# First S5 layer: block 0's table spread on TensorE, its loads first in GpSimd's queue, TensorE's opening in written order behind products of ones

## The chip, the cores and the metric

The kernel runs on one core of a Trainium2 chip. The metric is the device time of one execution in microseconds (us); the figure of a kernel is the median of its runs. The engines are TensorE (PE; its weight loads are PEld), VectorE (DVE), ScalarE (ACT), GpSimd (POOL) and SyncE (SP). SP issues most loads, GpSimd and ScalarE issue some, each in the order of its own queue.

## What is computed

A decoder trunk of four layers over 256 positions of width 1024. The token mixer of layers 0 and 3 is a diagonal complex state-space layer (S5), that of layer 1 attention with a forget gate, that of layer 2 gated linear attention. Each layer also has an MLP with squared ReLU and a gated per-layer embedding. Only the S5 layer at the start is touched:

```python
u = xn @ w_in                                  # xn = rmsnorm(h, norm_mix)
ab = exp(lam * dt)                             # complex, 64 groups x 64 states
coef = (ab - 1) / lam
x = einsum(u, coef * b)                        # into the states, per group of 16 channels
s = scan over time of s = ab * s + x
y = real(einsum(s, c)) + d_skip * u
z = gelu(y) @ w_glu;  h += ((z1 * sigmoid(z2)) @ w_out)
```

## The kernel before

All of it is float32. A float32 weight in `dense` is split by ScalarE into a rounded high part (`whi`) and by VectorE into a low part (`wlo`), and TensorE multiplies with both. In the first S5 layer the columns `u` are instead made with plain float32 products, which show as two records each in the trace.

The S5 layer treats four positions at a time. It has four *blocks* of 256 channels, and the work of block `b` is written as short steps, a letter and a number:

- `w(2b)`, `w(2b+1)`: the two halves of `u` of block `b`, eight products of 128x256 each. `w_in` comes in eight pieces (`halves`, loaded by `half` in turn into buffers named raw, wh, wl, so pieces 0, 3, 6 are named raw, pieces 1, 4, 7 wh, pieces 2, 5 wl). Odd pieces need the second half of the channels of x.
- `f(b)`: fetches the matrix b (`bT`) and the powers of `ab` for this block (`coef`, 64 copies of a small table spread over 128 partitions). The table is made once: VectorE computes `powers`, TensorE transposes them (`s5_table`), ScalarE copies them to the tile `ct`, four DMAs write `ct` to memory (`tab`), and two DMAs per block read it back spread out.
- `j(b)`: fetches `bc` (b and c for the way out).
- `i(b)`: VectorE multiplies bT with coef (`s5_in`: tiles `wh`, `wl`, three instructions, L865 to L867). `r(b)`: the rotation `rot`. `o(b)`, `k(b)`: the way out (`qo`, from `bc` and `cpow`) and the short-lag kernel `tm`, which goes through `kk` and DMAs.
- `u(b)`: VectorE scales the columns by the norm (`rstd`), and eight DMAs lay them out as `U`. `x(b)`: TensorE multiplies U with wh and wl, 64 written products. `s(b)`, `e(b)`: VectorE turns the result (tiles P, W, R) and scans. `y(b)`: TensorE adds tm, P and W parts. `t(b)`, `g(b)`: gelu and transposition.
- `d`, `l`, `a`, `b`: load and split pieces of `w_glu` and multiply the gate; `P`, `p`: products of the embedding (`praw`).

The norm needs the mean of squares: ScalarE makes `x` and `sq` of each of four pieces of h, TensorE adds them up (`mean`, L1258), VectorE adds epsilon (`rrow`, L337), GpSimd takes the power -0.5 (L341), VectorE makes `diag`, TensorE spreads it with a matrix of ones (L351), ScalarE copies it (`rstd`, L353).

The order on the engines is set by a scheduler with a simulated timeline: it takes the program's steps in the order of the strings FIRST and LATER as written and puts every instruction on its engine where that simulation has it ready. Two things bind it. `in_order` chains the instructions of the named engines inside its `with`. `keep_in_program_order` pins GpSimd's fetches. Buffers come from pools; "wt" (bT and coef) has four, "wk" in PSUM three.

Of the kernel before, what the change touches and what calls it, by code (L numbers as in the profile page):

```python
# [13 lines left out]
ALU = mybir.AluOpType  # L14
# [13 lines left out]
FIRST = """w2 w3 u0 r0 w4 i0 f2 x0 o0 j2 P0 k0 w5 u1 w6 s0 d0 e0 y0 r1 i1 f3 x1 t0 o1 j3 k1 g0 u2 w7 l0 P1 d1 s1 a0 p0 e1 y1 r2 i2 x2 t1 o2 k2 g1 u3 p1 p2 d2 p3 d3 l1 b0 l2 d4 a1  # L28
# [3 lines left out]


# [27 lines left out]
class Trunk:  # L61
# [767 lines left out]
    def s5_table(self, j, F):  # L829

        nc = self.nc
        ps = self.psum((128, 2, 128), "mk")
        nc.tensor.matmul(ps.rearrange("p i x -> p (i x)"), self.zero[:, 0:128], self.zero[:, 0:256], start=True, stop=True)
        for i in range(2):
            nc.tensor.transpose(ps[:, i, :], F[:, i].rearrange("x s p -> x (s p)"), self.ident)
        ct = self.a2("ct", (128, 2, 2, 64))
        nc.scalar.copy(ct.rearrange("x i g n -> x i (g n)"), ps)
        tab = self.dram.tile([2, 4, 4, 2, 8, 64], F32, name=f"tab{j}")
        for i in range(2):
            for g in range(2):  # L840
                nc.gpsimd.dma_start(tab[g, :, :, i].rearrange("s b p n -> (s b) p n"), ct[:, i, g, :])
        return tab


    def s5_fetch(self, j, tab, b, pin=lambda x: x):

        nc = self.nc
        bT, cf = (self.t4(n, (128, 2, 512), tag="wt") for n in ("bT", "coef"))
        pin(nc.gpsimd.dma_start(bT, self.A["s5_bT"][j, b]))
        for g in range(2):  # L850
            pin(nc.gpsimd.dma_start(cf[g * 64:(g + 1) * 64], tab[g, :, b].rearrange("s i p n -> s (i p n)").unsqueeze(0).broadcast_to([16, 4, 1024])))
        return bT, cf
# [6 lines left out]
    def s5_in(self, b, bT, cf, ahead=False):  # L859

        nc = self.nc
        if not ahead:
            w = [self.wp.tile([128, 2, 8, 64], F32, name=n, tag=n, bufs=BUFS[n]) for n in ("wh", "wl")]
            f = [t.rearrange("x i p n -> x i (p n)") for t in w]
            nc.vector.tensor_tensor(f[0], bT, cf[:, 0:1].broadcast_to([128, 2, 512]), ALU.mult)  # L865
            nc.vector.tensor_tensor(f[1][:, 0], bT[:, 0], cf[:, 1], ALU.mult)
            nc.vector.scalar_tensor_tensor(f[1][:, 1], bT[:, 1], -1.0, cf[:, 1], ALU.mult, ALU.mult)  # L867
            return [[w[0][:, 0], w[1][:, 1]], [w[1][:, 0], w[0][:, 1]]]
# [172 lines left out]
    def s5_ahead(self, l):  # L1041
# [8 lines left out]
        made = *self.s5_fetch(j, tab, 0), self.s5_fetch_out(j, 0)  # L1050
        yield
        parts = None
        for b in range(4):
# [9 lines left out]
            if b < 3:  # L1063
                made = *self.s5_fetch(j, tab, b + 1), self.s5_fetch_out(j, b + 1)
# [24 lines left out]
    def s5_start(self, l):  # L1089
# [7 lines left out]
        us, parts, rots, ins, outs, xs, states, Gs, units, bcs = ({} for _ in range(10))  # L1097
# [143 lines left out]
        if first:  # L1241
            halves = [self.raw0] + [self.half(w_in, i) for i in range(1, 8)]
            x = [self.t4("x", (128, 4, T), tag="x4") for _ in range(2)]
            x = [x[k // 4][:, k % 4] for k in range(8)]
            scalars, v["ms"] = self.s5_scalars(j), self.psum((128, 2))
# [15 lines left out]
            with self.in_order(mybir.EngineType.Activation):  # L1261
# [17 lines left out]
            run("f0 j0 f1 j1")  # L1279
            q.update(drain(scalars))  # L1280
            z(1)
            run("w1")
# [99 lines left out]
```

## Time and profile before

| | us |
|---|---|
| median of 3 runs | 1466.18 |
| lowest, highest | 1463.03, 1469.08 |
| profiled execution | 1464.28 |
| its span, first to last instruction | 1462.6 |
| first S5 layer, its block work on VectorE | about 31.5 to 126 of the span |
| TensorE busy, share of the span | 1400.6, 96% |
| VectorE, ScalarE, GpSimd busy | 1046.0, 717.6, 102.4 |

The profiled execution is 1.9 us below the median, and 1.7 us lie outside its span. Its mean granted TensorE clock is 0.985. Rows of the timeline give start, length, engine, line, operation, and in brackets the idle time ahead and what ended it.

### The profile page before, as it was taken

What the parts mean: (1) busy time and instruction counts of PE and PEld (TensorE: products, weight loads), DVE (VectorE), ACT (ScalarE), POOL (GpSimd) and SP (SyncE); (2) the same over time, 40 slices, a digit from 0 to 9 for tenths busy, and PEclk for the clock granted to TensorE, in tenths of its full rate; (3) what the DMA queues carried; (4) which work ended last, traced back from release to release, by engine and by line L of the source; (5) the groups of instructions that cost most, each with busy time, mean ns of one, the idle gap of its engine ahead of it and who ended that gap; (6) DMA issues with size and microseconds to landing.
All of it is one profiled execution on the core that took longest, in us unless ns stands there. A gap on an engine that the chain in (4) does not pass through costs nothing.

```text
span 1462.6 us, 26508 instructions
## 1 busy us (share of the span) xinstructions
PE 1400.6 (96%) x10718; PEld 1261.5 (86%) x10718; DVE 1046.0 (72%) x1651; ACT 717.6 (49%) x1117; POOL 102.4 (7%) x169
## 2 busy tenths in 40 slices
PE   8789999999999999999999999999997899999997
PEld 7688988888999888888989588888997799888897
DVE  7894678776777678786676468877676946766664
ACT  3224465454655665455566445455463345545453
POOL 3000000001010000100004000000002100000020
PEclk9999999999999999999999999999999899999999
DMA  7533556657554456765665445666656546566561
GB/s 259 151 104 113 179 170 201 188 162 223 177 150 145 121 167 189 251 211 178 188 181 155 130 129 187 196 210 191 216 161 206 175 148 185 176 185 197 174 191 58
DMA packets 143387, 255.06 MB, mean 174 GB/s; under 512 B 21680, under 2 KB 32272, under 8 KB 143264
## 3 DMA queue, kind: packets, MB, share of 16 engines
q1 hardware_dynamic: 129856, 227.66, 50.3%
q0 software_dynamic: 7520, 24.26, 4.9%
q10 hardware_dynamic: 5888, 1.44, 0.5%
q8 instruction: 84, 1.38, 0.4%
q14 instruction: 39, 0.32, 0.1%
HBM read 242.68 MB, written 7.86 MB: 171 GB/s over the span
## 4 chain that ended last, share of the span: by engine, by line
PE 59%; DMA 4%; DVE 3%; ACT 3%; issue 1%; POOL 1%; DVEq 0%; POOLq 0%; ACTq 0%; SPq 0%
PE wk L234 8%; PE acc L234 7%; PE wk L236 4%; PE wk L198 4%; PE wk L199 4%; PE wk L200 4%; PE acc L198 3%; PE acc L236 3%; PE acc L199 3%; PE acc L200 3%; PE mk L234 3%; PE po L234 2%; DMA raw<-mlp_w 2%; DVE wlo L181 2%; ACT whi L179 1%; PE mk L236 1%
## 5 line engine op out<-in xcount | busy, mean ns | idle before, releaser
L181 DVE TENSOR_TENSOR wlo<-raw,whi 128x1024 fp32r<-128x1024 f32 x404 | 491.4, 1225 | 289.1 <-ACT whi L179 284.8
L179 ACT CAST whi<-raw 128x1024 fp32r<-128x1024 f32 x404 | 420.0, 1049 | 498.1 <-DMA raw<-mlp_w 87.6
L234 PE MATMUL wk<-x,whi 128*128 128x512 f32 x576 | 182.0, 401 | 7.5 <-DVE relu L245 7.5
L236 PEld LDWEIGHTS wk<-x,wlo 128*128 128x128 f32 x576 | 106.8, 190 | 22.9
L234 PE MATMUL acc<-s,whi 128*128 128x512 f32 x384 | 118.9, 398 | 2.8 <-ACT whi L179 2.8
L236 PE MATMUL wk<-x,wlo 128*128 128x256 f32 x576 | 113.2, 281 | 0.0
L234 PEld LDWEIGHTS wk<-x,whi 128*128 128x128 f32 x576 | 92.1, 191 | 11.6 <-DVE relu L245 8.6
L198 PE MATMUL acc<-x,whi 128*128 128x256 f32 x352 | 99.8, 287 | 1.8 <-DVE u L1141 1.0
L200 PE MATMUL acc<-x,wlo 128*128 128x256 f32 x352 | 100.0, 286 | 0.8 <-DVE wlo L181 0.8
L199 PE MATMUL acc<-x,whi 128*128 128x256 f32 x352 | 99.4, 285 | 0.0
L236 PEld LDWEIGHTS acc<-s,wlo 128*128 128x128 f32 x384 | 70.5, 190 | 15.5
L234 PE MATMUL mk<-x,whi 128*128 128x512 f32 x256 | 81.4, 395 | 0.0
L236 PE MATMUL acc<-s,wlo 128*128 128x256 f32 x384 | 74.6, 283 | 0.0
L199 PE MATMUL wk<-s,whi 128*128 128x256 f32 x256 | 72.4, 283 | 0.0
L198 PE MATMUL wk<-s,whi 128*128 128x256 f32 x256 | 72.4, 283 | 0.0
L200 PE MATMUL wk<-s,wlo 128*128 128x256 f32 x256 | 72.3, 283 | 0.0
L198 PEld LDWEIGHTS acc<-x,whi 128*128 128x128 f32 x352 | 66.9, 191 | 3.3 <-issue 1.8
L200 PEld LDWEIGHTS acc<-x,wlo 128*128 128x128 f32 x352 | 67.3, 192 | 1.6 <-DVE wlo L181 1.3
L199 PEld LDWEIGHTS acc<-x,whi 128*128 128x128 f32 x352 | 67.2, 192 | 0.2
L234 PEld LDWEIGHTS acc<-s,whi 128*128 128x128 f32 x384 | 60.3, 190 | 4.7 <-ACT whi L179 3.0
L234 PE MATMUL po<-s,whi 128*128 128x512 f32 x192 | 60.3, 395 | 0.0
L234 PE MATMUL wk<-s,whi 128*128 128x512 f32 x192 | 59.2, 396 | 0.1
(394 smaller groups left out, 3356.7 us busy)
## 6 DMA issues: line engine op xcount, KB each, us to landing
raw<-mlp_w SPq DMA_DIRECT2D x256, 512.0 KB, 4.3
raw<-s_w_glu SPq DMA_DIRECT2D x32, 512.0 KB, 4.2
raw<-ple_gate SPq DMA_DIRECT2D x32, 512.0 KB, 3.7
raw<-fox_w_in SPq DMA_DIRECT2D x24, 512.0 KB, 3.8
raw<-gla_w_in SPq DMA_DIRECT2D x24, 512.0 KB, 3.9
raw<-s_w_out SPq DMA_DIRECT2D x16, 512.0 KB, 3.6
kept<-kept POOLq DMA_DIRECT2D x12, 512.0 KB, 4.7
raw<-s_w_in SPq DMA_DIRECT2D x11, 512.0 KB, 3.9
```

What stands on the lines that cost most here:

```text
L179: nc.scalar.copy(hi, raw)
L181: self.last_lo = nc.vector.tensor_tensor(lo, raw, hi.bitcast(F32), ALU.subtract)
L198: mm(ps, hi, x[:, 0], start=first, stop=False, skip_group_check=True)
L199: mm(ps, hi, x[:, 1], start=False, stop=False, skip_group_check=True)
L200: self.last_mm = mm(ps, lo, x[:, 0], start=False, stop=last, skip_group_check=True)
L234: mm(ps[n], hi[:, i, s], v[i], start=first and i == 0, stop=False, skip_group_check=True)
L236: self.last_mm = mm(ps[n][:, 0], lo[:, i, s], v[i][:, 0], start=False, stop=last and i == UK - 1, skip_group_check=True)
```

## The change

For block 0 the powers are no longer fetched from memory. `s5_pick` makes a 0/1 matrix from the identity on ScalarE, and `s5_spread` multiplies it with `ct` on TensorE into two PSUM buffers of "wk", from which VectorE reads them. Blocks 1 to 3 fetch theirs as before. The loads of bT of block 0, bc of block 0 and bT of block 1 are written first, and bc and the second bT are pinned in that order. `in_order` now holds TensorE too, around the opening: 14 products of ones, the means, `w(0)`, `w(1)`, the norm, the spread. FIRST begins with other steps.

```diff
-FIRST = """w2 w3 u0 r0 w4 i0 f2 x0 o0 j2 P0 k0 w5 u1 w6 s0 d0 e0 y0 r1 ...
+FIRST = """i0 w2 u0 w3 r0 x0 f2 w4 o0 j2 P0 s0 k0 w5 u1 w6 d0 e0 y0 r1 ...
+WARM = 14
...
+    def s5_spread(self, b):
+        out = []
+        for i in range(2):
+            ps = self.psum()
+            for p in range(8):
+                for g in range(2):
+                    self.nc.tensor.matmul(ps[g * 64:(g + 1) * 64, p * 64:(p + 1) * 64], self.pick[:, p], self.ct[:, i, g, :], start=True, stop=True, skip_group_check=True)
+            out.append(ps)
+        return out
+
+    def s5_pick(self, b):
+        self.pick = self.t2("pick", (128, 8, 64))
+        nc, v = self.nc, self.ident.rearrange("x (s p) -> x p s", p=32)[:, b * 8:(b + 1) * 8]
+        nc.scalar.copy(self.pick.rearrange("x p (c s) -> x p c s", s=4), v.unsqueeze(2).broadcast_to([128, 8, 16, 4]))
...
         def f(b):
             if first:
-                parts[b] = self.s5_fetch(j, self.tab, b, self.tc.keep_in_program_order)
+                bT = bTs[b] if b in bTs else self.s5_fetch_in(j, b, self.tc.keep_in_program_order)
+                cf = self.s5_fetch_powers(self.tab, b, self.tc.keep_in_program_order) if b else None
+                parts[b] = bT, [cf[:, i] for i in range(2)] if b else self.s5_spread(b)
...
+            bTs = {0: self.s5_fetch_in(j, 0)}
+            j_(0)
+            bTs[1] = self.s5_fetch_in(j, 1, self.tc.keep_in_program_order)
             scalars, v["ms"] = self.s5_scalars(j), self.psum((128, 2))
...
-            with self.in_order(mybir.EngineType.Activation):
+            with self.in_order(mybir.EngineType.Activation, mybir.EngineType.PE):
+                warm = self.psum((128, 128), "po")
+                for _ in range(WARM):
+                    nc.tensor.matmul(warm, self.ones, self.ones, start=True, stop=True)
                 next(scalars)
                 mean(0, scaled(0))
                 next(scalars)
                 next(scalars)
                 mean(1, scaled(1))
-                sq = scaled(2)
-                next(scalars)
-                next(scalars)
-                sq = [sq, scaled(3)]
-            def between():
+                self.s5_pick(0)
+                sq = [scaled(2)]
+                def between():
+                    next(scalars)
+                    next(scalars)
+                    sq.append(scaled(3))
+                w(0, between)
                 for i in range(2):
                     mean(2 + i, sq[i])
                 z(0)
-            w(0, between)
-            run("f0 j0 f1 j1")
-            q.update(drain(scalars))
-            z(1)
-            run("w1")
+                w(1)
+                q.update(drain(scalars))
+                z(1)
+                f(0)
+            run("f1 j1")
```

In the order below, names are those of the steps above, shapes are those written, and xN counts neighbours alike.

On TensorE, at the start of the program, before:

```order
L833 LDWEIGHTS zero
L833 MATMUL mk<-zero 128x256
L1258 MATMUL wk<-mean,sq 128x1 x4
L1133 MATMUL acc<-x,raw 128x256 x8
L1258 MATMUL wk<-mean,sq 128x1 x4
L835 MATMUL mk<-ident,powers 128x128 x2
L1258 MATMUL wk<-mean,sq 128x1 x4
L1133 MATMUL acc<-x,wh 128x256 x2
L1133 MATMUL acc<-x,wl 128x256 x8
L1133 MATMUL acc<-x,wh 128x256 x2
L1258 MATMUL wk<-mean,sq 128x1 x4
L1133 MATMUL acc<-x,wh 128x256 x4
```

And now, from behind the second piece of the mean to the spread (ahead of it stand the 14 products of ones, eight products of the means, and the first half of piece 0):

```order
L838 MATMUL mk<-ident,powers 128x128 x2
L1157 MATMUL acc<-x,raw 128x256 x4
L1287 MATMUL wk<-mean,sq 128x1 x4
L949 LDWEIGHTS zero
L949 MATMUL mk<-zero 32x512
L1157 MATMUL acc<-x,wl 128x256 x7
L1287 MATMUL wk<-mean,sq 128x1 x4
L1157 MATMUL acc<-x,wh 128x256 x8
L1157 MATMUL acc<-x,wl 128x256
L1157 MATMUL acc<-x,raw 128x256 x5
L354 MATMUL wk<-diag,ones 128x256
L855 MATMUL wk<-ct,pick 64x64 x32
```

The transposition of the powers stands inside piece 0 now, the last part of the mean behind seven products of piece 2 (wl), and the diag product and the spread behind five products of piece 3 (raw).

On GpSimd, in the same part, from the table's writes to the second bc, before:

```order
L841 DMA tab_208<-ct 16x8x64 x4
L341 TENSOR_TENSOR rrow<-rrow,mhalf 128x2
L849 DMA bT<-s_bT 128x1024
L851 DMA coef<-tab_208 64x1x1024 x2
L856 DMA bc<-s_bc 128x512
L849 DMA bT<-s_bT 128x1024
L851 DMA coef<-tab_208 64x1x1024 x2
L856 DMA bc<-s_bc 128x512
```

And now, from the first fetch, at the place where the load of sd stood:

```order
L868 DMA bT<-s_bT 128x1024
L101 AFFINE_SELECT blk<-ones 128x1
L102 AFFINE_SELECT blk<-ones 128x1
L879 DMA bc<-s_bc 128x512
L868 DMA bT<-s_bT 128x1024
L722 DMA sd<-s_dT 32x32
L754 MEMSET powers 128x32
L755 MEMSET powers 128x32
L815 MEMSET F_305 128x32
L816 MEMSET F_305 128x32
L845 DMA tab_236<-ct 16x8x64 x4
```

Two bT and a bc are moved from behind the power of the norm to GpSimd's first microseconds; behind the table's writes the power follows, and then only the coef of block 1.

On VectorE, where block 0 begins, before:

```order
L887 TENSOR_TENSOR rot<-F_287,F_288 128x1024
L337 TENSOR_SCALAR rrow<-wk 128x2
L889 TENSOR_TENSOR rot<-rot,scratch 128x8x64
L890 TENSOR_TENSOR rot<-rot,scratch 128x8x64
L350 TENSOR_SCALAR diag<-ident,rrow 128x128 x2
L865 TENSOR_TENSOR wh<-bT,coef 128x1024
L866 TENSOR_TENSOR wl<-bT,coef 128x512
L867 SCALAR_TENSOR_TENSOR wl<-bT,coef 128x512
L1141 TENSOR_TENSOR u<-acc,rstd 128x2x64x4
L905 TENSOR_TENSOR qo<-bc,cpow 128x1280
L905 TENSOR_TENSOR scratch<-bc,cpow 128x1280
```

And now:

```order
L911 TENSOR_TENSOR rot<-F_304,F_305 128x1024
L913 TENSOR_TENSOR rot<-rot,scratch 128x8x64
L914 TENSOR_TENSOR rot<-rot,scratch 128x8x64
L1165 TENSOR_TENSOR u<-acc,rstd 128x2x64x4
L889 TENSOR_TENSOR wh<-bT,wk 128x1024
L929 TENSOR_TENSOR scratch<-bc,cpow 128x1280
L890 TENSOR_TENSOR wl<-bT,wk 128x512
L891 SCALAR_TENSOR_TENSOR wl<-bT,wk 128x512
L889 TENSOR_TENSOR wh<-bT,coef 128x1024
L890 TENSOR_TENSOR wl<-bT,coef 128x512
```

u stands ahead of the products with bT; rrow, diag and the first product of bc (qo) have gone forward into the table of F, further up.

On SyncE, in the same part, from the last piece of w_in to the first pieces of tm, before:

```order
L269 DMA wh<-s_w_in 128x4x256
L171 DMA raw<-ple_proj 128x2x512
L1208 DMA praw<-pT 128x2x256
L171 DMA raw<-s_w_glu 128x2x512
L963 DMA U<-u 128x1x64 x4
L171 DMA raw<-ple_proj 128x2x512
L171 DMA raw<-s_w_glu 128x2x512
```

And now:

```order
L272 DMA wh<-s_w_in 128x4x256
L1234 DMA praw<-pT 128x2x256
L174 DMA raw<-ple_proj 128x2x512
L987 DMA U<-u 128x1x64 x4
L174 DMA raw<-s_w_glu 128x2x512
L174 DMA raw<-ple_proj 128x2x512
```

The first piece of w_glu stands behind U of block 0 now.

On VectorE, between the last scan work of block 0 and the scan of block 1, before:

```order
L1003 TENSOR_TENSOR W<-R,rot 128x8x63
L181 TENSOR_TENSOR wlo<-raw,whi 128x1024
L905 TENSOR_TENSOR qo<-bc,cpow 128x1280
L985 TENSOR_TENSOR P<-wk,rot 128x1024
L985 TENSOR_TENSOR W<-wk,rot 128x1024
L181 TENSOR_TENSOR wlo<-raw,whi 128x1024
```

And now:

```order
L1027 TENSOR_TENSOR W<-R,rot 128x8x63
L1009 TENSOR_TENSOR P<-wk,rot 128x1024
L184 TENSOR_TENSOR wlo<-raw,whi 128x1024
L929 TENSOR_TENSOR qo<-bc,cpow 128x1280
L1009 TENSOR_TENSOR W<-wk,rot 128x1024
L184 TENSOR_TENSOR wlo<-raw,whi 128x1024
```

P of block 1 has moved ahead of the next qo.

More of the change, by code (lines that the diff above doesn't have):

```diff
@@ L1049, in s5_ahead @@
         tab = self.s5_table(j, q["powers"])
-        made = *self.s5_fetch(j, tab, 0), self.s5_fetch_out(j, 0)
+        made = self.s5_fetch_in(j, 0), self.s5_fetch_powers(tab, 0), self.s5_fetch_out(j, 0)
         yield
@@ L1063, in s5_ahead @@
             if b < 3:
-                made = *self.s5_fetch(j, tab, b + 1), self.s5_fetch_out(j, b + 1)
+                made = self.s5_fetch_in(j, b + 1), self.s5_fetch_powers(tab, b + 1), self.s5_fetch_out(j, b + 1)
         yield
@@ L1096, in s5_start @@
         v = {}
-        us, parts, rots, ins, outs, xs, states, Gs, units, bcs = ({} for _ in range(10))
+        us, parts, rots, ins, outs, xs, states, Gs, units, bcs, bTs = ({} for _ in range(11))
         gT = []
```

24 lines of the change are left out of this document (14 added, 10 removed).

## The prediction

> **What bounds the kernel now.** The page comes first: TensorE (PE) is busy for 96% of the span, so nearly everywhere it is the limit. The change touches the first S5 layer alone, so that layer has to be read by stages: busy times of each engine from the start to the end of its last scan.
>
> ```profile
> PE 1400.6 (96%) x10718; PEld 1261.5 (86%) x10718; DVE 1046.0 (72%) x1651; ACT 717.6 (49%) x1117; POOL 102.4 (7%) x169
> 0.00:8.00 8.00, 2.12 (x9) 1.83 (x10) 5.49 (x32) 6.28 (x14) 2.68 (x18) 1.00 0.66 194
> 8.00:14.50 6.50, 6.50 (x20) 5.28 (x20) 6.43 (x59) 1.43 (x3) 0.00 (x0) 1.00 1.08 378
> 26.00:31.50 5.50, 5.50 (x26) 4.56 (x25) 0.00 (x0) 0.37 (x1) 2.87 (x6) 1.00 0.90 273
> 31.55:42.79 11.24, 10.02 (x88) 8.38 (x89) 11.24 (x13) 2.96 (x7) 3.67 (x7) 1.00 1.03 309
> 42.79:61.52 18.73, 12.83 (x192) 10.57 (x189) 18.73 (x24) 4.07 (x7) 1.09 (x2) 0.82 0.54 163
> 65.99:97.77 31.78, 27.37 (x506) 23.97 (x501) 31.03 (x38) 9.76 (x21) 0.54 (x1) 1.00 0.23 63
> 97.77:126.20 28.43, 27.98 (x440) 26.48 (x441) 21.04 (x25) 10.35 (x17) 0.75 (x3) 0.94 0.46 137
> ```
>
> A row has the stretch, its length, then the busy time and count of PE, PEld, DVE, ACT and POOL, the granted clock, the DMA share and GB/s. VectorE (DVE) does nothing from 26.0 to 31.5, and from 31.55 to 61.52 it never stops (11.24 of 11.24, 18.73 of 18.73), then 31.03 of 31.78 us up to 97.77. So until then VectorE carries the layer, while TensorE has 1.2, 5.9 and 4.4 us free in those stretches. After 97.77 TensorE is full. Whatever lets VectorE begin its block work earlier moves all of this, if TensorE's free time can follow. One line of VectorE's waits, and the order of time around its pause, say why it stands still:
>
> ```profile
> DVE qo L905 <- PE mk L1021: 3.3, 1, 3.3
> 15.57 0.37 ACT L837 COPY ct<-mk 128x256 f32<-128x256 f32 x1 [5.67 <-PE mk L835]
> 16.25 2.12 POOL L841 DMA_DIRECT2D tab<-ct  x4 [0.47 <-ACT ct L837]
> 22.89 1.70 POOL L341 TENSOR_TENSOR rrow<-rrow,mhalf 128x2 f32<-128x2 f32 x1 [4.52 <-DVE rrow L337]
> 25.17 1.03 POOL L851 DMA_DIRECT2D coef<-tab  x2
> 23.33 0.67 DVE L890 TENSOR_TENSOR rot<-rot,scratch 128x512 f32<-128x512 f32 x1
> 24.62 0.58 DVE L350 TENSOR_SCALAR diag<-ident,rrow 128x128 f32<-128x128 f32 x2 [0.62 <-POOL rrow L341]
> 31.55 1.23 DVE L865 TENSOR_TENSOR wh<-bT,coef 128x1024 f32<-128x1024 f32 x1 [6.35 <-DMA coef<-tab]
> 33.90 1.04 DVE L1141 TENSOR_TENSOR u<-acc,rstd 128x512 f32<-128x512 f32 x1
> 34.79 1.47 DVE L905 TENSOR_TENSOR qo<-bc,cpow 128x1280 f32<-128x1280 f32 x1
> 42.79 1.21 DVE L181 TENSOR_TENSOR wlo<-raw,whi 128x1024 fp32r<-128x1024 f32 x1
> ```
>
> The table is ready on chip (ct) at 15.94. It goes to memory, and its fetch (coef) stands in GpSimd's queue behind the power for the norm, which ends at 24.59. So it lands at 31.5, and VectorE loses 6.35 us, bracketed in its row.
>
> **The change, part by part.** *The table of block 0.* Two fetches of 256 KB go; 32 small products on TensorE take their place, and VectorE reads them from PSUM. That costs VectorE nothing: the product with rot reads PSUM too and takes 1.22 us, the same as L865's 1.23. The 32 products are 64 records; the nearest row has 64 records of the same 64x64 shape in 2.08. The copy "pick" on ScalarE has the size of a square of 128x512, 0.61 us, between loads.
>
> ```profile
> 79.45 2.08 PE L1021 MATMUL mk<-qo,P 64*64 64x64 f32 x64
> 67.40 1.22 DVE L985 TENSOR_TENSOR P<-wk,rot 128x1024 f32<-128x1024 f32 x1
> 1.00 0.20 POOL L95 MEMSET ones<- 128x128 f32 x1
> 5.61 0.61 ACT L1252 ACTIVATE sq<-h 128x512 f32<-128x512 f32 x1
> ```
>
> *The early loads.* bT of block 0, bc, and bT of block 1 (512 + 256 + 512 KB, 1.31 MB) are issued from about 2 us on, where sd alone stood. They share the DMA engines with x and the eight pieces of w_in.
>
> ```profile
> bT<-s_bT POOLq DMA_DIRECT2D x4, 512.0 KB, 5.2
> wl<-s_w_in SPq DMA_DIRECT2D x2, 512.0 KB, 7.2
> 4.77 0.51 SPq L269 DMA_DIRECT2D wl<-s_w_in  x1
> ```
>
> At the 378 GB/s of the full stretch 1.31 MB are 3.5 us, the upper bound for the delay of what follows. The lower bound is 0: the first 8 us moved 194 GB/s, which leaves room for (378 - 194) x 8 = 1.47 MB. The loads flow from about 4 us on, when that room is half gone, and the engines are full from 8 us, so I take 3.0, near the upper bound. The third piece of w_in, issued at 4.77, lands at about 12.0 now and at 15.0 then. The Trainium skill, page "DMA: Bandwidth & Descriptors", section "Queues, rings and completion order", says that an engine takes turns between the queues it has work for, a packet at a time. By that, all 1.31 MB pass before the third piece of w_in, 3.5 instead of 3.0 us, and the sum below would be 0.5 us smaller; no row here shows the turns.
>
> *TensorE's written order.* The fourth piece of the mean now stands behind seven of the eight products on the third piece of w_in. A warm 128x256 product is two records of 0.226 us (16 in 3.62), a cold one 0.404 (16 in 6.47).
>
> ```profile
> 8.00 6.47 PE L1133 MATMUL acc<-x,raw 128*128 128x256 f32 x16
> 24.07 3.62 PE L1133 MATMUL acc<-x,raw 128*128 128x256 f32 x16
> 21.45 0.95 PE L1258 MATMUL wk<-mean,sq 128*128 128x1 f32 x8
> 16.39 0.21 DVE L702 TENSOR_TENSOR prod<-F 128x32 f32<-128x32 f32 x1
> 17.31 0.43 DVE L703 TENSOR_TENSOR F<-F,prod 128x64 f32<-128x64 f32 x2
> ```
>
> So the means end at 15.0 + 14 x 0.226 + 0.95 = 19.1 (22.4 now). rrow on VectorE now stands in the middle of the F table, at the work that runs at 16.39, which comes 1.47 later since one product of bc (qo, at 34.79 now) is moved ahead of it: 17.9. VectorE waits 1.2 us there. Then diag: from the start of GpSimd's power to diag it takes 24.62 - 22.89 = 1.73 us, and some 0.1 before it; about 1.1 is covered by table work (16.39 to 17.5), so another 0.7. Stalls together: 1.9 us; between 0 (no delay of loads) and 2.4.
>
> *VectorE's new start.* The rotation of block 0 ends at 24.0 now. Then: 24.0 + 1.47 (qo) + 0.58 (diag, which now stands ahead of it) + 1.9 = 27.95. u follows at once if rstd is there. TensorE after the means: 16 + 2 + 10 records are 6.3 us, so 25.4; the diag product 0.4, so 25.8; rstd by 26.5. The spread ends at 25.9 + 2.1 = 28.0, before u ends at 28.8 (0.89 from u to the next row). The work from there to the row at 42.79 is 42.79 - 31.55 - 1.47 = 9.77 us, so that point comes at 37.7: **5.1 us earlier**. What hides the 2.1 us of the spread is u and the rotation; without them it would cost up to 2.1.
>
> *The second gap.* Once more VectorE waits 3.3 us to overwrite qo, until y of block 0 is done on TensorE. In the new order the product P of block 1 (1.22, of which the next row overlaps 0.1) stands ahead of that wait, since 35 in place of 19 of block 1's input products precede y. **1.1 us more.**
>
> *TensorE's debts.* Three projection products (6 records, 1.4 us) are moved from a stretch where TensorE idles to just before the first gate products; the 4.4 us idle in 65.99:97.77 hide them. The 14 products of ones need only the ones, ready at 1.2. They are 28 records of half the length, so even if all are cold they end by 1.2 + 28 x 0.202 = 6.9, when x is only half there; free. The gain of 16 x 0.178 = 2.8 us on the first piece of w_in is hidden behind loads.
>
> The sum is 5.1 + 1.1 = 6.2 us of the profiled execution: 1464.3 - 6.2 = 1458.1. The median of the three runs lies 1.9 above that execution, so the forecast of the median is **1460.0 us**, 0.4% less. The runs spread over 6 us, and 0.5% (7.3 us) is what can be told from no change; this gain falls just short of it.
>
> **The rivals.** *More comes of it.* If the loads fit into the room of the first 8 us, the 1.9 us of stalls go. And the slow gate products after 97.77 may go too: they follow a short wait of TensorE, which an earlier VectorE would change.
>
> ```profile
> 97.77 0.39 PE L198 MATMUL acc<-g,whi 128*128 128x256 f32 x1 [2.00 <-DVE W L1002]
> 97.99 0.28 PE L199 MATMUL acc<-g,whi 128*128 128x256 f32 x1
> 99.99 0.41 PE L198 MATMUL acc<-g,whi 128*128 128x256 f32 x1
> 100.21 0.41 PE L199 MATMUL acc<-g,whi 128*128 128x256 f32 x1
> 58.35 2.93 PE L446 MATMUL wk<-praw,raw 128*128 128x256 f32 x6
> ```
>
> Records there start 0.21 apart against 0.12 two microseconds before, about 16 of them, 1.5 us. Together 6.2 + 1.9 + 1.5 = 9.6, so 1456.6. For it: the second full stretch is full of TensorE work alone. Against it: the DMA share of 1.08 from 8.0 on.
>
> *The gain is eaten by w_glu.* On SyncE's queue the first load of w_glu stood ahead of U and now stands behind it. U is issued when u ends (28.8) and takes 2.6 us, so the load goes out at 31.4, not 27.72.
>
> ```profile
> 27.72 0.37 SPq L171 DMA_DIRECT2D raw<-s_w_glu  x1
> 34.97 2.60 SPq L963 DMA_DIRECT2D U<-u  x4
> 38.78 1.04 ACT L179 CAST whi<-raw 128x1024 fp32r<-128x1024 f32 x1
> raw<-s_w_glu SPq DMA_DIRECT2D x32, 512.0 KB, 4.2
> ```
>
> VectorE reaches its part of that piece at 38.8 (37.7 + 1.1). With the median 4.2 us to land, the copy ends at 36.7: hidden. If it took the 11 us that lie between issue and copy now, it would end at 43.5, and VectorE would wait 4.7: 1.5 us are left, 1464.7. In the new order the DMA engines have less to do there, since two bT are already in.
>
> *Slower: TensorE stays cold.* All its early steps now stand in one order, so slow products delay the norm with no way round. In the stretch where TensorE has 5.9 us free the granted clock is 0.82, and the six records at 58.35 took 0.49 each. If TensorE waits for x and w_in from 6.9 to about 10 after the products of ones, its clock may fall back. Up to rstd 58 large records stand in the order, at 0.18 more each 10.4 us, and the 64 small ones behind, 2 us: the block work would start about 12 us later than in my sum, and the change would lose 6: about 1472. It decides from 35 cold records on (6.2 / 0.18). Against it: now the 16 records from 8.00 are slow and the 16 from 24.07 are not, with no idle time between, so a cold start has cost some 16 records, 2.8 us, much of it behind loads. The Trainium skill, page "TensorE: Matmul & The Clock Gate", section "What's actually happening", has the clock rise after about 3.4 us of work and fall after an idle window as long; a pause of 3.1 us would then mostly keep it. The slow records from 98.95 on, after a wait of 2.0 us, speak against the page, so I keep a small chance.
>
> **How the numbers follow.** Forecast (3 to 7.3 us gained, 1458.9 to 1463.2): 0.54. More: 0.30, of which a little stays under 0.5%. Eaten by w_glu or by longer load delays (0 to 3 us): 0.12. Slower: 0.04, half of it over 0.5%. The range takes in 9.6 us and some 2.6, near half the spread of the runs, at the fast end (1454.0), and a gain of next to nothing at the slow end (1467.0). Faster by over 0.5%, that is under 1458.8: 0.32; within 0.5%: 0.65; slower: 0.03.
>
> **What would show it.** Right: VectorE has no wait for coef in block 0; its first product with bT starts near 28.7; rrow waits 1 to 2 us for the means; the row of w_glu's low part at 42.79 comes near 38.8; the end of the last block's VectorE work moves from 126.2 to about 120. Wrong: the third piece of w_in after 16; VectorE waiting for whi near 39; TensorE products of w_in at 0.4 each after 10 us; or an S5 stage shorter by 6 us whose gain is gone by the MLP.

## The result and the profile after

The changed kernel takes 1456.55 us in the median of six runs (1454.13 to 1458.21), the kernel before 1465.8 beside it: ratio 0.994, 95% interval 0.992 to 0.996. The same kernel run once more, twelve times, gave 0.9955 (0.994 to 0.997), so by the two medians the gain is 0.45 to 0.6%, 6.6 to 8.8 us. The profiled executions took 1464.28 and 1458.21, 6.07 apart; the profiled one is the slowest of the six, and what the medians have more fits scatter of that kind.

The first S5 layer ends when ScalarE loads its table for the gates. That row of the timeline, and the window up to it (columns as in the prediction), of before:

```profile
133.96 1.28 ACT L1229 ACT_TABLE_LOAD   x1
...
0.00:133.96 133.96, 114.75 (x1649) 101.96 (x1649) 105.26 (x222) 39.15 (x78) 17.01 (x46) 0.96 0.51 155
```

And of after:

```profile
127.62 1.28 ACT L1255 ACT_TABLE_LOAD   x1
...
0.00:127.62 127.62, 115.98 (x1741) 104.22 (x1741) 105.55 (x222) 40.02 (x79) 15.15 (x44) 0.99 0.52 159
```

The end comes 6.34 us sooner. What follows it takes 1330.3 us in the one profile (1464.28 - 133.96) and 1330.6 in the other: between these two profiles all of the difference is in this layer. VectorE does the same work in both, 222 instructions in 105.3 and 105.6 us. So the layer is as long as that work and VectorE's idle time, which falls from 28.7 to 22.1 us; it is counted in this way for every kernel below. Its waits up to the end of the last block (total, times, longest), of before those that the prediction didn't show (one of 1.0 us for `tm` is in both):

```profile
DVE wlo L181 <- ACT whi L179: 6.6, 2, 4.4
DVE W L985 <- PE wk L975: 1.2, 2, 0.6
DVE cs L748 <- ACT sh L740: 1.0, 1, 1.0
```

All of after:

```profile
DVE wlo L184 <- ACT whi L182: 5.9, 4, 3.0
DVE rrow L340 <- PE wk L1287: 4.9, 1, 4.9
DVE tm L113 <- PEq L1409: 1.0, 1, 1.0
DVE W L1009 <- PE wk L999: 0.8, 2, 0.6
DVE cs L751 <- ACT sh L743: 0.7, 1, 0.7
DVE qo L929 <- PE mk L1045: 0.2, 1, 0.2
```

The wait of 6.35 us for coef is gone, and one of 4.9 for the means is new: a net 1.5. The wait ahead of the second qo went from 3.3 to 0.2 (3.1), whi gave 0.7, diag 0.6, and W and cs together 0.7. That makes the 6.6 us.

The wait for the means begins at TensorE. Its timeline after, and VectorE's, in the stretches that the prediction spoke of:

```profile
1.25 5.02 PE L1294 MATMUL po<-ones 128*128 128x128 f32 x28 [1.25 <-POOL ones L98]
7.96 1.05 PE L1287 MATMUL wk<-mean,sq 128*128 128x1 f32 x8 [0.60 <-ACT sq L1281]
11.87 3.49 PE L1157 MATMUL acc<-x,raw 128*128 128x256 f32 x8 [2.85 <-DMA raw<-s_w_in]
15.77 1.89 PE L1157 MATMUL acc<-x,raw 128*128 128x256 f32 x8
21.82 0.95 PE L1287 MATMUL wk<-mean,sq 128*128 128x1 f32 x8
29.28 2.08 PE L855 MATMUL wk<-ct,pick 128*64 128x64 f32 x64
...
22.81 0.16 DVE L340 TENSOR_SCALAR rrow<-wk 128x2 f32<-128x2 f32 x1 [4.88 <-PE wk L1287]
23.97 0.47 DVE L353 TENSOR_SCALAR diag<-ident,rrow 128x128 f32<-128x128 f32 x2
30.75 1.04 DVE L1165 TENSOR_TENSOR u<-acc,rstd 128x512 f32<-128x512 f32 x1
31.65 1.20 DVE L889 TENSOR_TENSOR wh<-bT,wk 128x1024 f32<-128x1024 f32 x1
41.72 1.21 DVE L184 TENSOR_TENSOR wlo<-raw,whi 128x1024 fp32r<-128x1024 f32 x1
62.87 1.49 DVE L929 TENSOR_TENSOR qo<-bc,cpow 128x1280 f32<-128x1280 f32 x1 [0.19 <-PE mk L1045]
...
12.60 0.91 ACT L1279 ACTIVATE x<-h,gains 128x256 f32<-128x256 f32 x2 [3.72 <-DMA h<-xT]
```

TensorE waits 2.85 us for the first piece of w_in, which it used from 8.00 on before, and runs the first eight records at 0.44 us each, where the next eight take 0.24. The means end at 22.8, rrow stands until then, and block 0's first product starts at 31.65 us. Before, it started at 31.55: the wait that was removed bought this product nothing. The third piece of h came late too: ScalarE takes it at 12.60, where before took it at 8.47. That cost nothing further here, since TensorE is busy with w_in without a gap from 11.87 until the means have ended.

At the other end of the layer TensorE's gate products begin at 92.73 instead of 97.77, and are no longer slow (the granted clock is the third number from the end, 0.94 before):

```profile
92.73:119.81 27.08, 26.63 (x442) 25.11 (x441) 23.39 (x30) 10.24 (x17) 0.75 (x3) 1.00 0.50 149
```

From the first of them to the end of VectorE's last block it takes 27.08 us, 28.43 before.

### The profile page after: what moved, and what is told of

Same layout as the page of the kernel before. It is cut to its first block, busy times and chain, and to the rows that moved or that the text cites. A ratio compares the mean times of both kernels' runs of the same rounds, so it can differ in the third digit from the quotient of the medians.

```text
span 1456.2 us, 26681 instructions
## 1 busy us (share of the span) xinstructions
PE 1401.7 (96%) x10810; PEld 1264.3 (87%) x10810; DVE 1046.4 (72%) x1651; ACT 717.2 (49%) x1118; POOL 100.9 (7%) x167
## 4 chain that ended last, share of the span: by engine, by line
PE 63%; DMA 2%; DVE 2%; ACT 2%; issue 0%; DVEq 0%; POOLq 0%; ACTq 0%; SPq 0%
PE wk L237 8%; PE acc L237 7%; PE wk L239 4%; PE wk L201 4%; PE wk L202 4%; PE wk L203 4%; PE acc L201 4%; PE acc L202 3%; PE acc L203 3%; PE acc L239 3%; PE mk L237 3%; PE po L237 2%; PE acc L262 1%; PE acc L261 1%; PE acc L263 1%; PE mk L239 1%
```

## The experiments

All ratios are to the kernel before, run beside each kernel, with 95% intervals. "End" is the load of the gates' table, "idle" VectorE's idle time up to it, both of one profiled execution. An edit also lets the scheduler place other instructions elsewhere, so each row tells of a program as it was scheduled anew. The other FIRST alone moves nothing: with the old one the programs of all five engines are the same.

| kernel | loads of bT and bc | block 0's table | ones | TensorE's order | ratio | end | idle |
|---|---|---|---|---|---|---|---|
| before | GpSimd, late | memory | no | free | 1 | 133.96 | 28.7 |
| after | GpSimd, first | spread | 14 | written | 0.994 (0.992 to 0.996) | 127.62 | 22.1 |
| e1 | GpSimd, first | spread | 14 | written | 0.9955 (0.994 to 0.997) | 129.86 | 24.2 |
| e2 | SyncE | spread | 14 | written | 0.992 (0.9895 to 0.994) | 124.42 | 19.1 |
| e3 | GpSimd, first | memory | 14 | written | 0.994 (0.992 to 0.996) | 129.65 | 24.3 |
| e4 | GpSimd, first | spread | no | written | 0.9975 (0.996 to 0.999) | 132.66 | 26.6 |
| e5 | GpSimd, first | spread | 14 | free | 1.005 (1.003 to 1.007) | 141.09 | 34.8 |
| e6 | SyncE | memory | no | free | 0.993 (0.992 to 0.994) | 124.73 | 19.4 |
| e7 | SyncE | spread | no | written | 0.9925 (0.991 to 0.994) | 128.99 | 23.4 |
| e8 | SyncE | memory | 14 | written | 0.992 (0.990 to 0.994) | 127.17 | 22.0 |
| e9 | GpSimd, first | memory | no | free | 0.995 (0.993 to 0.997) | 127.25 | 21.4 |
| e10 | GpSimd, late | spread | 14 | written | 0.995 (0.993 to 0.997) | 126.31 | 20.9 |
| e11 | SyncE | spread | 14 | free | 0.995 (0.994 to 0.997) | 128.84 | 23.3 |
| e12 | GpSimd, first | spread | 14 + 8 | written | 0.993 (0.991 to 0.994) | 123.10 | 17.7 |

The row of windows from which "idle" is taken, of e12:

```profile
0.00:123.10 123.10, 116.43 (x1757) 106.12 (x1757) 105.38 (x222) 40.01 (x78) 15.13 (x44) 1.00 0.53 165
```

VectorE's work is 105.2 to 106.3 us in each. The idle time saved, divided by 1464, gives the ratio to within 0.004: e5 has 6.1 us more and is 0.5% slower, e12 has 11.0 less, 0.75%, and is 0.7% faster. But 0.004 is half of the largest gain. What follows the layer takes from 1323.4 us (e7) to 1331.6 (e1) in the fourteen profiled executions, so "end" and "idle" show where a layer's time goes, and the ratio shows what a kernel is worth.

### The changed kernel again (e1)

No edit.

> The changed kernel once more, unaltered. The profiled executions of the two kernels are 6.1 us apart (1464.3 and 1458.2), and all of it lies before the end of the first S5 layer (gelu table load for w_glu at 133.96 and 127.62); the medians are 9.2 us apart. Theory A (the S5 layer is all, the rest of the 9.2 is scatter of the runs): ratio to the kernel before 0.9955 to 0.9965, 5 to 6.5 us. Theory B (something behind the layer, such as the other order in the GLA layer, gives 3 us more): ratio 0.993 to 0.9945, 8 to 10 us.

Ratio 0.9955, median 1456.27 (1453.4 to 1463.25) against 1463.23. That is the fast end of theory A; the interval, 0.994 to 0.997, doesn't shut out theory B. Its profile has the same shape: TensorE waits 1.56 us for w_in, VectorE 4.1 for the means. The layer's end moves by 2.2 us between two profiles of one program, so a difference of 2 us in that column says little by itself.

### Who holds up w_in: the loads on SyncE's queue (e2)

```diff
-            bTs = {0: self.s5_fetch_in(j, 0)}
-            j_(0)
-            bTs[1] = self.s5_fetch_in(j, 1, self.tc.keep_in_program_order)
+            bTs = {i: self.t4("bT", (128, 2, 512), tag="wt") for i in range(2)}
+            bcs[0] = self.g2("bc", (128, 4, 8, 16))
+            nc.sync.dma_start(bTs[0], A["s5_bT"][j, 0])
+            nc.sync.dma_start(bcs[0], A["s5_bc"][j, :, 0])
+            nc.sync.dma_start(bTs[1], A["s5_bT"][j, 1])
```

The three loads stand behind the eight pieces of w_in there.

> The two bT and the bc of the start are loaded through SyncE's queue behind the eight pieces of w_in, not through GpSimd's ahead of them. Theory A (the early loads hold up x and w_in, and so the 4.9 us wait of VectorE for the means at rrow): the first product of w_in starts at 8 to 9 us in place of 11.9, the means end near 18.5 in place of 22.8, VectorE's wait at rrow falls below 1.5 us, and the S5 layer ends 1 to 4 us earlier than with the change (TensorE is 98% busy in its second half, so not the full 4). Total 1452 to 1456. Rival (the wait at rrow comes from TensorE's written order or its cold clock, not from the loads): the wait at rrow stays 4 to 5 us, total 1456 to 1459.

Ratio 0.992, median 1452.22 (1448.66 to 1456.49); the changed kernel, run beside it on the same chip, had 1456.27. The means are 4.9 us apart, with a standard error of 1.5. Its timeline:

```profile
8.98 1.97 PE L1157 MATMUL acc<-x,raw 128*128 128x256 f32 x8
18.82 0.48 DVE L353 TENSOR_SCALAR diag<-ident,rrow 128x128 f32<-128x128 f32 x2
25.99 1.03 DVE L1165 TENSOR_TENSOR u<-acc,rstd 128x512 f32<-128x512 f32 x1
26.88 1.20 DVE L889 TENSOR_TENSOR wh<-bT,wk 128x1024 f32<-128x1024 f32 x1
```

The first piece of w_in is used at 8.98 without a wait and at full speed, rrow doesn't wait for the means, and block 0 starts at 26.88 instead of 31.65. So the wait of 4.9 us came with the early loads in GpSimd's queue, by the late pieces and by the slow records behind them, which are missing here as well (e12 takes the two apart). This kernel beats both.

### The loads alone, in the old kernel (e9 and e6)

The kernel before, with only the loads of bT (blocks 0, 1) and bc (block 0) moved: first in GpSimd's queue (e9), or to SyncE behind w_in (e6).

```diff
+            bTs.update({i: self.t4("bT", (128, 2, 512), tag="wt") for i in range(2)})
+            bcs[0] = self.g2("bc", (128, 4, 8, 16))
+            nc.gpsimd.dma_start(bTs[0], A["s5_bT"][j, 0])      # e6: nc.sync
+            nc.gpsimd.dma_start(bcs[0], A["s5_bc"][j, :, 0])
+            nc.gpsimd.dma_start(bTs[1], A["s5_bT"][j, 1])
...
-            run("f0 j0 f1 j1")
+            run("f0 f1 j1")
```

> The kernel before, with the table by memory, no ones and its old order, in which bT of blocks 0 and 1 and bc of block 0 are loaded by SyncE's queue behind the eight pieces of w_in instead of by GpSimd behind the table. Theory: the wait for bc in front of qo (3.3 us) is what this takes away, and the wait for coef (6.35 us) stays, since only the table sets it; some of qo's work can move into it. Ratio 0.995 to 0.998, less than the 0.992 of the changed kernel with the same loads on SyncE. Rival: the loads are everything, and the spread, the ones and TensorE's order nothing: ratio 0.990 to 0.994, like that kernel. A second rival: nothing is gained, since the wait for coef takes up what qo's wait gives back: 0.9985 to 1.001.

> The kernel before, with the table by memory, no ones and TensorE's old order, in which bT and bc are loaded first in GpSimd's queue as the change does it: the loads' part of the change alone. Theory: the loads in themselves hold up x and the first pieces of w_in by 3 to 4 us, and without the written order the third and fourth mean wait behind w_in's late products, so that the gain from an early bc (0.993 with the same loads on SyncE) is spent: ratio 0.997 to 1.005. Rival: the old kernel has enough slack in front of its wait for the table (6.35 us) to take a late w_in, and the loads early by either queue are the whole gain: ratio 0.992 to 0.9955.

0.993 and 0.995. In both, the rival that gave the loads the whole gain was right, and my theory wrong. (The expectation of e6 calls the wait of 3.3 us one for bc. By its row in the prediction it is a wait for TensorE, mk, and e6 still has 2.3 us of it.) Before, the first bc was used as soon as it landed, at 31.98, too late for any work on qo inside the pause. Its row, and VectorE's timeline of e9, which shows what I had missed:

```profile
31.98 0.40 ACT L916 ACTIVATE bx<-bc,blk 128x128 f32<-128x128 f32 x1 [1.29 <-DMA bc<-s_bc]
...
26.43 1.48 DVE L907 TENSOR_TENSOR scratch<-bc,cpow 128x1280 f32<-128x1280 f32 x1
27.95 0.82 DVE L910 TENSOR_TENSOR qo<-qo,scratch 128x640 f32<-128x640 f32 x1
30.27 1.23 DVE L867 TENSOR_TENSOR wh<-bT,coef 128x1024 f32<-128x1024 f32 x1 [0.76 <-DMA coef<-tab]
```

With bc there early, the work on qo that stood behind the wait at 34.79 moves into it. The table still comes through memory and is used 1.3 us sooner, at 30.27, with no bT ahead of it in the queue; 0.76 us of the 6.35 are left to wait for it. The pause need not be shortened; it can be filled.

### Everything but the loads (e10)

The changed kernel with the three loads behind the table's writes in GpSimd's queue.

```diff
-            bTs = {0: self.s5_fetch_in(j, 0)}
-            j_(0)
-            bTs[1] = self.s5_fetch_in(j, 1, self.tc.keep_in_program_order)
...
                 w(0, between)
+                bTs = {0: self.s5_fetch_in(j, 0, self.tc.keep_in_program_order)}
+                j_(0)
+                bTs[1] = self.s5_fetch_in(j, 1, self.tc.keep_in_program_order)
```

> The changed kernel with the spread, the ones and the written order, in which bT and bc are put behind the table's writes in GpSimd's queue, as the kernel before had them: the change without the part of the loads. Theory: w_in comes early again and the means with it, but bc lands late, at about 24 us as before or later, so that qo's two large products cannot fill the time ahead of u, and bT for the first block's product is late as well: the wait of 3.3 us in front of qo is back. Ratio 0.995 to 0.999. Rival: with the spread, ones and order the late loads fit behind VectorE's work, and the kernel is as fast as with them on SyncE's queue: 0.9905 to 0.994.

0.995, at the fast end of the theory. The late bc costs what it was to cost, in part:

```profile
28.44 1.49 DVE L929 TENSOR_TENSOR qo<-bc,cpow 128x1280 f32<-128x1280 f32 x1 [1.08 <-DMA bc<-s_bc]
```

The wait for TensorE ahead of a later qo is back too, 3.6 us. Here w_in is on time and qo waits for bc; in the changed kernel it is the other way round. The loads alone give 0.995, the rest alone 0.995, and both together 0.994 to 0.9955. The parts do not add: each by itself takes nearly all of the wait for coef (0.8 us is left in e9, none in e10). The new wait for the means isn't the whole reason, since without it the loads alone (e6, 0.993) and everything together (e2, 0.992) are as close.

### The table by memory again (e3, and e8 with the loads on SyncE)

```diff
-                cf = self.s5_fetch_powers(self.tab, b, self.tc.keep_in_program_order) if b else None
-                parts[b] = bT, [cf[:, i] for i in range(2)] if b else self.s5_spread(b)
+                cf = self.s5_fetch_powers(self.tab, b, self.tc.keep_in_program_order)
+                parts[b] = bT, [cf[:, i] for i in range(2)]
...
-                self.s5_pick(0)
```

> Block 0's table goes through memory as before; the early loads, the products of ones and TensorE's written order stay. Theory A (the wait for the table was only one of several limits, since with the change block 0's first product starts at 31.65 as before): VectorE does u and the products of bc first, waits for coef at most 1 to 2 us, and the total is within 3 us of the changed kernel, 1456 to 1460. Rival (the spread is what gives the gain): a wait of 4 us or more for coef is back and the total is 1461 to 1466.

> The changed kernel with bT and bc on SyncE's queue behind w_in, and block 0's coefficients by memory again instead of by the spread. Theory: with the loads out of the way the table is what the first block waits for: in the kernel before it landed at 31.55 us, while with the spread the block's first product began at 26.9; VectorE has u, rot and qo to put into that gap, about 4 us of qo's work, so 0 to 2 us are lost: ratio 0.992 to 0.9935 and the last block's end at 124 to 127 us. Rival one: the wait for the table is back in full (4 to 6 us), and the spread is worth that once the loads are early: ratio 0.994 to 0.997. Rival two: the table lands earlier too, since its writes and reads no longer stand behind the early loads in GpSimd's queue, and nothing is lost: 0.9905 to 0.992.

e3 has 0.994, the changed kernel's own ratio; e8 0.992, the ratio of e2. VectorE shows no wait for coef in either. Block 0's first product comes behind u and the work on qo. Its row in the timeline of e3:

```profile
34.49 1.22 DVE L889 TENSOR_TENSOR wh<-bT,coef 128x1024 f32<-128x1024 f32 x1
```

In e8 it stands 3 us sooner:

```profile
31.46 1.22 DVE L889 TENSOR_TENSOR wh<-bT,coef 128x1024 f32<-128x1024 f32 x1
```

So the spread itself, the change's main part, is worth nothing that these runs can tell, with bc early. e8's later end (127.17 against 124.42 in e2) isn't the table's alone: in its profile the first eight records of w_in were slow, 3.38 us against 1.97, and VectorE waits 1.7 us for the means (the last section comes back to it). e8's time lies in the range of the theory; that nothing at all is lost, as its second rival had it, isn't excluded.

### Without the ones (e4, and e7 with the loads on SyncE)

```diff
-                warm = self.psum((128, 128), "po")
-                for _ in range(WARM):
-                    nc.tensor.matmul(warm, self.ones, self.ones, start=True, stop=True)
```

> Without the 14 products of ones. In the changed kernel TensorE waits 2.9 us for w_in behind them and the first four products of w_in then take 0.436 per record, as cold as without. Theory A (the ones are wasted or nearly): total within 2 us of the changed kernel; the products of w_in are cold up to about 16 to 18 us. Rival (the ones are what warms TensorE by 15 us): products of the third piece of w_in at 0.42 per record, the means end 3 us later, VectorE's wait at rrow grows to 7 or 8 us, total 1459 to 1462.

> The changed kernel with bT and bc on SyncE's queue behind w_in, and without the 14 products of ones. Theory: with w_in no longer late, TensorE goes from the ones straight to the means and w_in's products, which ran in 1.97 us for eight records; without the ones they run cold, at about 3.5 us for eight, as in the kernel before, so that the means, u and the first block come 1.5 to 3 us later than with the ones. Ratio 0.993 to 0.9945 against 0.9918 with them, and the last block's end at 126 to 128 us against 124.4. Rival: VectorE's own chain of powers sets when u can begin, and the ones are worth nothing here: ratio 0.9905 to 0.993, end at 123 to 126 us.

e4 has 0.9975, 3 to 5 us slower than the changed kernel, and e7 0.9925, the same as e2 within the intervals. TensorE's timeline of e7:

```profile
6.44 3.55 PE L1289 MATMUL wk<-mean,sq 128*128 128x1 f32 x16 [6.44 <-ACT sh L743]
9.85 3.76 PE L1157 MATMUL acc<-x,raw 128*128 128x256 f32 x8
```

The slow start was as expected, 3.76 us for the eight records against 1.97 in e2, and the measured ratio fits the rival, while the end at 128.99 fits neither. The two part because what follows the layer took 1323.4 us in that profile, 7 less than before's; why it was shorter is left open. e4's total is the rival's, but not for its reasons: the means ended at 21.45, sooner than in the changed kernel, and VectorE's wait for them shrank. In e4 VectorE's order changed too: it waits 1.3 us for the means and 5.4 ahead of the second qo, so its loss can't be put on the clock.

### The pause filled (e12)

```diff
                 mean(1, scaled(1))
+                for _ in range(8):
+                    nc.tensor.matmul(warm, self.ones, self.ones, start=True, stop=True)
                 self.s5_pick(0)
```

> The changed kernel with eight more products of ones on TensorE, in written order between the second mean and the first product of w_in, where TensorE stood for 2.85 us and then ran its first eight records of w_in in 3.49 us. Theory: the pause is what let the clock fall; the 16 records of ones fill some 2 us of it, the first eight records of w_in take about 2.0 us, and the means, rrow and the first block come 1.5 us earlier: ratio 0.992 to 0.995, with the last block's end about 1 to 3 us before the 127.6 and 129.9 us of the two profiles of the changed kernel. Rival one: TensorE is as slow after the ones as after the pause (3.3 us or more for the eight records), and the kernel stays at 0.994 to 0.9965. Rival two: the eight records are fast, but the time stays, because VectorE's wait for the means only moves to a later wait: 0.994 to 0.9965 as well, told apart from rival one by the eight records alone.

0.993, median 1452.4 (1450.62 to 1456.85), and its timeline:

```profile
9.09 2.03 PE L1301 MATMUL po<-ones 128*128 128x128 f32 x16
10.97 1.99 PE L1157 MATMUL acc<-x,raw 128*128 128x256 f32 x8
18.60 0.95 PE L1287 MATMUL wk<-mean,sq 128*128 128x1 f32 x8
```

And the wait that was 4.9 us, in its waits:

```profile
DVE rrow L340 <- PE wk L1287: 0.4, 1, 0.4
```

As the theory had it: with the pause filled the eight records take 1.99 us instead of 3.49 (that a pause is needed for them to be slow isn't so, as the last section shows). The last mean ends 3.2 us sooner (19.55 against 22.77): 0.9 of it is w_in, begun at 10.97 here and at 11.87 there, 1.5 the faster records, and the rest the order behind them. VectorE's wait for it falls from 4.9 to 0.4, the remaining 1.3 since rrow now stands later in the table's work. By its end and idle time it is the shortest layer of all; by its ratio it can't be told from e2.

### TensorE's order free (e5, and e11 with the loads on SyncE)

```diff
-            with self.in_order(mybir.EngineType.Activation, mybir.EngineType.PE):
+            with self.in_order(mybir.EngineType.Activation):
```

> The changed kernel with the ones, the spread table and the early loads kept, but TensorE's first steps no longer held in written order (ScalarE's still are). Theory: the written order gives nothing by itself; what sets the start of the first block are the pieces of x and w_in that come late behind the early loads, whichever order TensorE takes them in. Then the ratio to the kernel before stays at 0.994 to 0.9965, and the last block's end (the load of ScalarE's table of functions for the gates) stays at 127 to 131 us of the span. Rival: the written order brings the four means forward and so the spread table; without it u and the table's product come later by the 3 to 4 us that the third and fourth mean lose, and the ratio is 0.997 to 1.000, with that mark at 132 or later.

> The changed kernel with bT and bc on SyncE's queue behind w_in, spread and ones kept, but TensorE's first steps not in written order. Theory: the written order is worth what the late w_in would otherwise cost; with w_in on time the third and fourth mean come soon enough in either order, and the loss of 10 us that the free order showed with the loads first on GpSimd shrinks to 0 to 3 us: ratio 0.9915 to 0.994. Rival: the order by itself costs the time, since diag and u stand behind three pieces of w_in's products and the spread behind diag: ratio 0.996 to 1.002.

e5 is slower than the kernel before, 1.005 (1.003 to 1.007): the theory was wrong, and the loss larger than the rival's. e11 has 0.995, between its two ranges. The timeline of e5:

```profile
24.71 0.16 DVE L340 TENSOR_SCALAR rrow<-wk 128x2 f32<-128x2 f32 x1 [4.61 <-PE wk L1287]
34.19 0.59 PE L354 MATMUL wk<-diag,ones 128*128 128x256 f32 x2
34.72 2.09 PE L855 MATMUL wk<-ct,pick 128*64 128x64 f32 x64
40.09 1.21 DVE L889 TENSOR_TENSOR wh<-bT,wk 128x1024 f32<-128x1024 f32 x1
```

One of its waits, 5.9 us after:

```profile
DVE wlo L184 <- ACT whi L182: 10.0, 4, 4.1
```

The third and fourth mean stand among w_in's products again, the product with diag at 34.19, and the spread behind it. Block 0 starts 8.4 us later than after. e9 has the same loads and the same free order, but takes the table from memory and has no ones; its block 0 starts at 30.27, ahead of u, since nothing of it needs TensorE. The spread ties block 0 to TensorE's queue, and with it the order becomes worth 11 to 13 us of the layer (141.09 against 129.86 and 127.62); that it is the spread and not the ones is read from these rows, and no run took it alone.

## Why the prediction was right, and where not

The sum for the profiled execution was 6.2 us, 1464.3 to 1458.1; measured were 6.07, 1458.21. The 1.9 us added for the median went the wrong way: the profiled run after lies 1.7 above its median, and the forecast of 1460.0 is 3.45 above the measured 1456.55. The 9.25 us between the medians are not the forecast's case (3 to 7.3 us) but that of the rival "more", 1456.6, with its chance of 0.30; the repeat, 7.0 us, and the profiles are in the forecast's. But the terms of the sum were not right, and two errors cancelled.

- *The wait for coef is gone.* So it is. But I put that on the spread; e3 loses the wait as well, and e9 all but 0.8 us of it, by filling it.
- *The early loads, 3.0 us.* This is the step that failed. I followed the third piece of w_in and took the first for hidden ("The gain of 16 x 0.178 = 2.8 us on the first piece of w_in is hidden behind loads"). TensorE stood at the first: it was used from 8.00 on before, and from 11.87 after, 3.9 us later and beyond the bound of 3.5. In e1 it was used at 11.05 and in e9 at 11.25, 3.1 and 3.3 later (rows below). The third piece was as late (10.7 us from issue to landing instead of 7.2, so at 15.9 instead of 12.0), but nothing waited for it. So 3.0 was somewhat small, and it was put on the wrong piece. The Trainium skill ("DMA: Bandwidth & Descriptors", "Queues, rings and completion order") has an engine take turns between its queues, a packet at a time; the prediction's estimate by that, 3.5 us, was for the third piece. The delays scatter around it and tell no turns apart.
- *Stalls at rrow and diag, 1.9 us, between 0 and 2.4.* Measured 4.9 and 0. To the late piece came the slow (cold) records, 3.49 us for eight against 1.9. The means ended at 22.8, not 19.1.
- *u at 27.95, first product at 28.8, spread hidden.* 30.75, 31.65, and hidden: all 2.8 late, as the stalls are 3.0 too small. Without the hold-up e2 has 25.99 and 26.88.
- *The row of w_glu's low part near 38.8.* 41.72, late by the same 2.9; it moved by 1.1 us from 42.79, not by 4.0.
- *The second gap, 1.1 us.* 3.1. Nearly the whole wait went, but 0.9 of it only moved to a wait for whi just ahead (61.46), and 0.9 came because TensorE had y done 4.1 us after the last product W of block 0's scan began (58.75), where it took 5.1 before (60.93). Neither was forecast.
- *More comes of it.* Half of this rival came true: the gate products are warm and the stretch is 1.35 us shorter (forecast 1.5). Its other half, no stalls, turned into the opposite.
- *w_glu.* Its first piece did not delay VectorE, as the sum had it: the row at 41.72 has no wait.
- *TensorE stays cold.* Its condition came true: TensorE waited for w_in behind the ones and the clock fell back, but for some eight records and not for 35.
- *The signs.* No wait for coef, and an end of VectorE's last block at 119.81 (about 120 was forecast). The starts near 28.7 and 38.8 and the 1 to 2 us at rrow did not come, and one sign of being wrong did: products of w_in at 0.44 us a record after 10 us.

The 3.0 us too little for the stalls were made up by 2.0 more at the second qo and by smaller waits, 0.7 at whi and 0.7 at W and cs, less 0.3 of work more. That the total came out right is luck in its parts; what carries it is that VectorE's work is constant and its idle time sets the layer.

The clock is worth its rows (windows of after; the granted clock stood at 0.50 from 12.00 to 14.50):

```profile
9.10:11.80 2.70, 0.00 (x0) 0.00 (x0) 2.67 (x26) 0.00 (x0) 0.00 (x0) 0.95 1.03 366
11.80:15.40 3.60, 3.53 (x9) 2.61 (x9) 3.56 (x21) 2.60 (x7) 0.00 (x0) 0.56 1.09 381
```

A granted 0.95 over 2.70 us and 0.56 over 3.60 are, at half speed, 0.27 and 3.17 us: the clock was down for 3.4 us, from about 11.5 to 15. The Trainium skill ("TensorE: Matmul & The Clock Gate", "What's actually happening") has a free-running window of about 3.4 us for the rise, and the trace agrees. It asks as long a window of idleness for the fall. Here the fall came 2.5 us after the last mean had ended at 9.0 and 5.2 after the ones had, so whether less was enough hangs on whether the one-column means hold the clock. e8 (last section) shows that they did not, and that there 2.1 us behind the ones were enough.

## What to carry to other kernels

When an engine waits, look first for work of its own that could stand in the wait, and ask which load keeps it from being there: moving three loads gave what the rest of the change gave, and both together gave no more. Loads that are put first are paid for by the loads that were first; behind w_in on its own queue they cost VectorE no wait for the means in e2 (0.992 against 0.994 to 0.9955). Warming products that end well before the data comes are in part lost, so let them reach to it, and where a step is moved onto a busy engine, its order there must be settled too.

## What the runs showed of the hardware that I had not expected

After products from 1.25 to 9.0, TensorE's clock fell in a pause of 2.85 us, and with 16 more records of ones in that pause it did not (1.99 against 3.49 us for eight records). The same records in e1:

```profile
11.05 3.29 PE L1157 MATMUL acc<-x,raw 128*128 128x256 f32 x8 [1.56 <-DMA raw<-s_w_in]
```

In e9, with the window around them:

```profile
11.25 3.78 PE L1136 MATMUL acc<-x,raw 128*128 128x256 f32 x8 [3.10 <-DMA raw<-s_w_in]
...
11.20:15.00 3.80, 3.75 (x10) 3.00 (x10) 3.77 (x23) 2.60 (x7) 0.00 (x0) 1.00 1.09 382
```

In e1 a pause of 1.56 us, with one of 1.1 ahead of the second mean, already did it. In e9, which has no ones, the eight records are as slow at 0.47 each, and yet the granted clock stands at 1.00, as it does for before's slow 16 records from 8.00. It seems that the column shows no throttle ahead of the first change of the clock; at the start of a trace the time of a record says more than the clock.

No pause ahead of w_in is needed at all. e2 and e8 have the same opening on TensorE, with a gap of 0.59 us and no wait for w_in. In e2 the eight records take 1.97 us, in e8 3.38. The second mean of e2, then the same stretch of e8 with the window around it:

```profile
8.07 1.05 PE L1289 MATMUL wk<-mean,sq 128*128 128x1 f32 x8 [0.59 <-ACT sq L1283]
...
7.99 1.32 PE L1289 MATMUL wk<-mean,sq 128*128 128x1 f32 x8 [0.59 <-ACT sq L1283]
9.18 3.38 PE L1157 MATMUL acc<-x,raw 128*128 128x256 f32 x8
8.50:12.00 3.50, 3.50 (x12) 2.96 (x13) 3.46 (x33) 1.43 (x3) 0.00 (x0) 0.52 1.09 384
```

A granted 0.52 over 3.50 us is 3.4 us at half speed, so the clock fell at about 8.6, in the middle of the second mean and 2.1 us after the ones had ended at 6.5: the one-column products did not hold it. What orders the runs with ones is the time from the end of the ones to the first product of w_in: 5.6 us in the changed kernel, 5.2 in e5, 4.7 in e1, 3.5 in e3 and 2.7 in e8, all slow; 2.6 in e2, 2.4 in e11, 1.5 in e10 and none in e12, all fast. Between e8 and e2 lie 0.03 us, so between those two something else decides, and no run tells what.
